# A hybrid decoder step on one core: the third k tile moves into the first array, and the squares of x are taken two chunks later

## The chip, the core and the metric

The kernel runs on one core of one Trainium2 chip. The metric is the device time of one execution in microseconds (us). Three executions of the kernel before took 1296.19, 1296.63 and 1296.79 us; the median is 1296.63 us.

## What is computed

One inference step of a one-layer decoder trunk for 264 tokens (256 of a prompt and 8 samples) with a model width of 2048. What matters here is the beginning:

```python
def rms_norm(x, g):
    xf = x.astype(jnp.float32)
    y = xf * lax.rsqrt(jnp.mean(xf * xf, axis=-1, keepdims=True) + EPS)
    return (y * g.astype(jnp.float32)).astype(x.dtype)

    xn = rms_norm(x, g_mix)
    z = xn @ w_in                     # 2048 x 3584, split among three mixers
    u_pool, u_lru, u_gel, c_a, c_b = z[..., :c0], z[..., c0:c1], ...
    # pooling mixer, RG-LRU mixer, conformer mixer: y_pool, y_lru, y_conf
    gates = jax.nn.sigmoid(xn @ w_gate + b_gate)
    x = x + (g_a * y_pool + g_b * y_lru + g_c * y_conf) @ w_out
    hid = jnp.square(jax.nn.relu(rms_norm(x, g_mlp) @ w_up))
    x = x + hid @ w_down              # then a last rms_norm
```

Everything is in float32. The outputs are the normalized tokens and the new states of the mixers.

## The kernel before, in words

**Three matmuls for one.** Every product is made from operands split in two: a weight block of 128 x 1024 is loaded into one of 6 buffers of `raw`, ScalarE (ACT) casts it to the rounded half `whi` (L176), and VectorE (DVE) subtracts that to get the rest `wlo` (L177). `whi` and `wlo` have 4 buffers each. TensorE (PE) then computes whi·x_hi, whi·x_lo and wlo·x_hi (L199 to L201). x has 16 k tiles of 128 features by 264 tokens; each is scaled by `g_mix` and split in two the same way into `A` (L298 on ACT, L299 on DVE).

**Chunks.** All weights form one list of chunks, and one Python loop runs over it: at chunk i, PE multiplies chunk i, while the splits of chunk i + 3 and of the x tiles that it needs are written out just ahead. Chunks 0 to 3 are the "wide" ones (one k tile by 1024 columns of `w_in`, 24 matmuls each, L981); from chunk 4 on a chunk is two k tiles by 512 columns, also 24 matmuls. Chunks 4 to 9 and 10 to 15 finish the same 1024 columns for the other 12 k tiles; when chunk 9 is done, four result banks are copied off by ACT (L400). The order on each engine is the order in which the loop writes the instructions out (a list of delayed functions, `later(n, fn)`, is emptied at the end of each chunk's turn); each engine runs its own list strictly in that order.

**Transfers.** All are issued by SyncE's queue (SP) in order. At first come four pieces of the array `head_dram`, which holds `g_mix` and, for k tiles 0 and 1, x and the weight row one behind the other (tile `first`, L160); then x tile 2 from `x_dram` (L157) and chunk 2 in two halves from `wall_dram` (L154), then x tiles and chunks in turn. From chunk 8 on, two chunks come in one transfer of 1 MB (L147; the pair of chunks 12 and 13 is one), which waits until DVE has read the buffers that it overwrites.

**The norm's factor.** Since the scale 1/rms belongs to a token, it is applied to results of `w_in`, not to x. For it, ACT squares x in four groups of four tiles (`x_squares`, L334; the first group in two instructions), DVE adds the groups (L338) and folds four tiles to one (L345, L346), `rms_parts` folds the 128 partitions in two halves with DVE and ACT in turn (L277, L278, L285, L281) into `parts`, and one matmul with a matrix of ones sums over the partitions (`sum_mm`, L273). That matmul is written into PE's list in the middle of chunk 13 (`if i == 13 and kt == 1: x_rms()`). Its result goes through Ln and Exp on ACT (L257) and four steps on DVE to `rstd`.

Of the kernel before, what the change touches and what calls it, by code (L numbers as in the profile page):

```python
# [16 lines left out]
P = 128  # L17
# [3 lines left out]
N = TP + TS  # L21
KD = D // P
# [24 lines left out]
CH = 1024  # L47
# [3 lines left out]
WARM = 7 * (512,)  # L51
AHEAD = 3
EARLY = 2
SINGLE = 1
WIDE = 4
TAIL = 6
# [4 lines left out]
ROW = N + CH  # L61
# [31 lines left out]
def hybrid_step(ctx: ExitStack, tc: tile.TileContext, head_in, x_in, par_in, st_in, row_in, wall, y_out, c_out, st_out):  # L93
    nc = tc.nc
# [8 lines left out]
    raw = cpool.tile([P, NRAW, CH], F32, name="raw")  # L103
    whi = cpool.tile([P, NHI, CH], F32R, name="whi")
    wlo = cpool.tile([P, NHI, CH], F32R, name="wlo")
    qtmp = cpool.tile([P, 16 * N], F32, name="qtmp", tag="Q")
    first = cpool.tile([P, KD + EARLY * ROW], F32, name="first")
    early = first[:, KD:].rearrange("p (k c) -> p k c", k=EARLY)
    X = cpool.tile([P, KD, N], F32, name="X")
# [4 lines left out]
    par = cpool.tile([P, NPAR], F32, name="par")  # L114
    st = cpool.tile([P, S_OUT], F32, name="st")
# [9 lines left out]
    def pv(name, i=None, n=1):  # L125
        a, b = PCOL[name]
        return par[:, a:b] if i is None else par[:, a + i:a + i + n]

    def acc():
        return psum.tile([P, 512], F32, name="acc", tag="acc")  # L130
# [11 lines left out]
    def dma_pair(p):  # L142
        s = (2 * p) % NRAW
        if p >= n_pairs:
            return
        if chunks[2 * p][3] == chunks[2 * p + 1][3] == CH and p < n_pairs - SINGLE:
            nc.sync.dma_start(raw[:, s:s + 2, :], wall[p].rearrange("p (a c) -> p a c", a=2))  # L147
        else:
            for h in range(2):
                if chunks[2 * p + h][3]:  # L150
                    dma_part(2 * p + h, 0, chunks[2 * p + h][3])

    def dma_part(c, a, b):
        nc.sync.dma_start(raw[:, c % NRAW, a:b], wall[c // 2, :, c % 2 * CH + a:c % 2 * CH + b])  # L154

    def dma_x(a, b):
        nc.sync.dma_start(X[:, a:b, :], x_in[:, a - EARLY:b - EARLY, :])  # L157

    def dma_first(a, b):
        nc.sync.dma_start(first[:, a:b], head_in[:, a:b])  # L160
# [1 line left out]
    def x_tiles(a, b):  # L162
        return early[:, a:b, :N] if b <= EARLY else X[:, a:b, :]

# [5 lines left out]
    def split(j, a=0, b=CH):  # L170
        if j >= len(chunks) or not chunks[j][3]:
            return
        h, lo = in_two(j)
        s = slice(a, min(b, chunks[j][3]))
        r = early[:, j, N + s.start:N + s.stop] if j < EARLY else raw[:, j % NRAW, s]
        nc.scalar.copy(h[:, s], r)  # L176
        nc.vector.tensor_tensor(lo[:, s], r, f(h[:, s]), op=ALU.subtract)  # L177
# [43 lines left out]
    def later(n, fn):  # L221
        delayed.append((now[0] + n, fn))
# [26 lines left out]
    def spend(**kw):  # L249
        for e, c in kw.items():  # L250
            credit[e] -= c
# [61 lines left out]
    warm, one = acc(), nc.const_aps.tensor(1.0, (P, P), BF16)  # L313
    for n in WARM:
        nc.tensor.matmul(warm[:, :n], one, nc.const_aps.tensor(1.0, (P, n), BF16), start=True, stop=True)
    for c, a, b in ((2, 2, 3), (3, 3, 4), (4, 4, 6), (5, 6, 8), (6, 8, 10), (7, 10, 12)):
        dma_x(a, b)
        for u, v in ((0, 512), (512, CH)) if c == 2 else ((0, CH),):
            dma_part(c, u, v)
    el = B[0].rearrange("p a n -> p (a n)")[:, :8 * (TP + 3)].rearrange("p (a n) -> p a n", a=8)  # L320
    nc.gpsimd.memset(el[:, :, 0:3], 0.0)
    nc.gpsimd.memset(vext[:, :, 0:30], 0.0)
# [4 lines left out]
    def x_tile(k):  # L327
        split_scaled(A[:, k, :], A[:, 16 + k, :], x_tiles(k, k + 1)[:, 0, :], first[:, k:k + 1], k < 2)

    def x_squares(j):  # L330

        t = sq4 if j == 0 else G[:, 4 * (j % 2):4 * (j % 2) + 4, :]
        for a, b in ((0, EARLY), (EARLY, 4)) if j == 0 else ((0, 4),):
            nc.scalar.activation(t[:, a:b, :], x_tiles(4 * j + a, 4 * j + b), AF.Square)  # L334
        spend(act=1.1)

        def add():
            nc.vector.tensor_tensor(sq4, sq4, t, op=ALU.add)  # L338
            spend(dve=1.25)

        if j:
            later(1, add)
# [11 lines left out]
    def softplus():  # L354
        sc = G[:, 8, :]
        t0, t1, t2, w, t4 = (sc[:, 8 * i:8 * i + 8] for i in range(5))
        lam = pv("lru_lambda")
        nc.scalar.activation(t0, lam, AF.Abs)
        nc.scalar.activation(w, t0, AF.Exp, scale=-1.0)
        nc.vector.tensor_scalar(t0, w, 2.0, None, op0=ALU.add)  # L360
        nc.vector.reciprocal(t1, t0)
        nc.vector.tensor_scalar(t4, lam, -1.0, 0.0, op0=ALU.mult, op1=ALU.max)
        eng = nc.gpsimd
        eng.tensor_tensor(t0, w, t1, op=ALU.mult)
        eng.tensor_tensor(t1, t0, t0, op=ALU.mult)
        terms = 10
        eng.memset(t2, 2.0 / (2 * terms + 1))
        for i in range(terms - 1, -1, -1):
            eng.tensor_tensor(t2, t2, t1, op=ALU.mult)
            eng.tensor_scalar(t2, t2, 1.0, 2.0 / (2 * i + 1), op0=ALU.mult, op1=ALU.add)  # L370
        eng.tensor_tensor(t2, t2, t0, op=ALU.mult)
        eng.tensor_tensor(t2, t2, t4, op=ALU.add)
        eng.tensor_scalar(sp[:, 0:8], t2, 4.0, 0.0, op0=ALU.mult, op1=ALU.add)
        eng.tensor_scalar(sp[:, 8:16], t2, -8.0, 0.0, op0=ALU.mult, op1=ALU.add)
# [600 lines left out]
    def wide_mm(k):  # L975

        hi, lo = whi[:, k % NHI, :], wlo[:, k % NHI, :]
        for ms in ((0, 1), (2, 3), (4, 5), (6, 7)) if k == 0 else (range(4), range(4, 8)):
            for w, x, start in ((hi, k, True), (hi, KD + k, False), (lo, k, False)):
                for m in ms:  # L980
                    nc.tensor.matmul(pair[m][:, :N], w[:, m * P:(m + 1) * P], sent(A[:, x, :]),  # L981
                                     start=start and k == 0, stop=False)

    def x_of(i):

        return [i] if i < WIDE else range(2 * i - WIDE, min(2 * i - WIDE + 2, KD))
# [17 lines left out]
    for i, ch in enumerate(chunks):  # L1004
        now[0] = i
        for k in x_of(i + AHEAD):
            x_tile(k)
        for a in (0, 512) if i < 3 else (0,):
            if i + AHEAD < len(chunks) - 1:
                split(i + AHEAD, a, a + (512 if i < 3 else CH))  # L1010
        if i == end - 2:
            split(len(chunks) - 1)
        if ch[0] == "wide":
            wide_mm(i)
        if i == 16:
            softplus()
            nc.gpsimd.tensor_scalar(gfin, pv("g_final"), -0.5, 0.0, op0=ALU.mult, op1=ALU.add)
        if i == 0:
            dma_x(12, 16)
        if i % 2 == 0:  # L1020
            dma_pair((i + 8) // 2)
        if i == 3:
            nc.sync.dma_start(par, par_in)
            nc.sync.dma_start(st[:, :S_IN], st_in)
        kind, gi, c, _ = ch
        if kind == "dense":
            rhs, fn = group(gi)
            n = groups[gi][2] // 2
            if i >= end:
                run_bg()  # L1030
                continue
            if c == 0:
                pss = [acc() for _ in range(4)] if gi > 2 else pair[4 * gi - 4:4 * gi]
                if groups[gi][:2] == ("w_down", 48) and groups[gi][3] == 3:
                    end_tiles()
            if i < end - 2:
                for kt in range(2):
                    if i == 13 and kt == 1:
                        x_rms()
                    for m in range(4):  # L1040
                        tile_mm(i, gi, c, kt, m, rhs, pss, c == n - 1 and kt == 1)
            elif i == end - 1:
                for m in range(4):
                    for b in range(4):
                        tile_mm(i - 1 + b // 2, gi, c - 1 + b // 2, b % 2, m, rhs, pss, b == 3)
            if c == n - 1:
                for m in range(4):
                    fn(m, pss[m])
                after(gi)
        elif kind == "lru":  # L1050
            for j in range(2):
                lru_gate_mm(2 * gi + j, i, j)
            if gi == 3:
                lru_tail()
        elif kind == "grp":
            grp_mm(i)
        if i == end - 2:
            nc.scalar.preload_act_table_set(ROOT)
        if i == 140:
            nc.sync.dma_start(st_out, st)  # L1060
        if end - 20 <= i < end - 4:
            for n in range(2):
                dma_turned(2 * (i - end + 20) + n)
        if end - 4 <= i < end:
            dma_rows(i - end + 4)
        if 5 <= i < 9:
            x_squares(i - 5)
        if i == 9:
            later(0, x_sum)
            later(1, lambda: rms_parts(sq4[:, 0, :]))  # L1070
        run_bg()
# [285 lines left out]
```

## Time and profile before

| what | us |
|---|---|
| median of three runs | 1296.63 |
| the profiled execution itself | 1296.88 |
| its span, first to last instruction | 1295.2 |
| PE busy | 1289.7 |
| DVE busy | 835.8 |
| ACT busy | 720.0 |

The profile is of one execution; its granted TensorE clock is 0.999. In the views, a row of the timeline gives the start, the duration, the engine, the line of the kernel and the tiles, and in brackets how long the engine had been idle and what released it. Instructions of one engine overlap by a little, so the distance from one start to the next is what an instruction costs its engine. The 1.7 us between the span and the time of the execution lie outside the instructions.

### The profile page before, as it was taken

To read this page: it belongs to the slowest core of one execution; us is meant where nothing else is said; L and a number is where in the kernel's file an instruction comes from. 1 tells how busy PE (TensorE), PEld (TensorE's weight loads), DVE (VectorE), ACT (ScalarE), POOL (GpSimd) and SP (SyncE) were. 2 spreads that over 40 slices of the span, in tenths; PEclk is the share of its full clock that TensorE was granted. 3 is DMA by queue.
4 is the path that set the end of the run, shared out by engine and by line. 5 is a ranking of instruction groups with operands and counts; after the bars stand their busy time and mean duration, and the time that the engine had idled before them with its cause. 6 is when DMAs were issued, how large, how long until landed. Compare 5 with 4: busy or idle time off the path is not lost.

```text
span 1295.2 us, 26872 instructions
## 1 busy us (share of the span) xinstructions
PE 1289.7 (100%) x11460; PEld 1286.1 (99%) x11460; DVE 835.8 (65%) x1064; ACT 720.0 (56%) x1034; POOL 122.1 (9%) x170
## 2 busy tenths in 40 slices
PE   9999999999999999999999999999999999999998
PEld 8999999999999999999999999999999999999998
DVE  6896898776776677666655455655455645465654
ACT  7767677667675655455544334543344533354455
POOL 0250010110102023131000000000000000001033
PEclk9999999999999999999999999999999999999999
DMA  9656566555565554655555555555555555555672
GB/s 342 219 184 203 186 212 201 196 196 195 197 228 195 192 197 162 229 195 195 197 195 196 196 196 195 196 196 196 195 196 195 196 195 196 195 196 196 207 221 93
DMA packets 44743, 257.91 MB, mean 199 GB/s; under 512 B 9824, under 2 KB 10848, under 8 KB 15312
## 3 DMA queue, kind: packets, MB, share of 16 engines
q1 hardware_dynamic: 44624, 256.21, 58.1%
q8 instruction: 89, 1.46, 0.4%
q14 instruction: 30, 0.25, 0.1%
HBM read 252.36 MB, written 3.22 MB: 197 GB/s over the span
## 4 chain that ended last, share of the span: by engine, by line
PE 99%; DMA 0%; DVE 0%; ACT 0%; issue 0%; DVEq 0%
PE acc L201 33%; PE acc L200 32%; PE acc L199 32%; PE acc L981 1%; PE acc L1103 1%; DMA first<-head_dram 0%; PE acc L1122 0%; DVE G L1200 0%; PE acc L1137 0%; DVE end L1190 0%; PE acc L273 0%; ACT whi L176 0%; PE acc L1118 0%; PE acc L1132 0%; DVE end L1173 0%
## 5 line engine op out<-in xcount | busy, mean ns | idle before, releaser
L177 DVE TENSOR_TENSOR wlo<-raw,whi 128x1024 fp32r<-128x1024 f32 (+2 forms) x479 | 585.3, 1224 | 439.4 <-ACT whi L176 433.6
L176 ACT CAST whi<-raw 128x1024 fp32r<-128x1024 f32 (+2 forms) x479 | 492.7, 1032 | 525.2 <-PE acc L200 479.2
L201 PE MATMUL acc<-A,wlo 128*128 128x264 f32 x1952 | 538.9, 276 | 0.0
L200 PE MATMUL acc<-A,whi 128*128 128x264 f32 x1952 | 538.8, 276 | 0.0
L199 PE MATMUL acc<-A,whi 128*128 128x264 f32 x1952 | 538.7, 276 | 0.0
L201 PEld LDWEIGHTS acc<-A,wlo 128*128 128x128 f32 x1952 | 368.9, 189 | 0.1
L199 PEld LDWEIGHTS acc<-A,whi 128*128 128x128 f32 x1952 | 368.9, 189 | 0.0
L200 PEld LDWEIGHTS acc<-A,whi 128*128 128x128 f32 x1952 | 368.9, 189 | 0.0
L199 PE MATMUL acc<-xn,whi 128*128 128x264 f32 x1024 | 282.6, 276 | 0.0
L200 PE MATMUL acc<-xn,whi 128*128 128x264 f32 x1024 | 282.6, 276 | 0.0
L201 PE MATMUL acc<-xn,wlo 128*128 128x264 f32 x1024 | 282.6, 276 | 0.0
L199 PEld LDWEIGHTS acc<-xn,whi 128*128 128x128 f32 x1024 | 193.5, 189 | 0.0
L201 PEld LDWEIGHTS acc<-xn,wlo 128*128 128x128 f32 x1024 | 193.5, 189 | 0.0
L200 PEld LDWEIGHTS acc<-xn,whi 128*128 128x128 f32 x1024 | 193.5, 189 | 0.0
L200 PE MATMUL acc<-Q,whi 128*128 128x264 f32 x620 | 171.1, 276 | 0.0
L199 PE MATMUL acc<-LH,whi 128*128 128x264 f32 x616 | 170.0, 276 | 0.0
L201 PE MATMUL acc<-LH,wlo 128*128 128x264 f32 x616 | 170.0, 276 | 0.0
L200 PEld LDWEIGHTS acc<-Q,whi 128*128 128x128 f32 x620 | 117.2, 189 | 0.0
L199 PEld LDWEIGHTS acc<-LH,whi 128*128 128x128 f32 x616 | 116.4, 189 | 0.0
L201 PEld LDWEIGHTS acc<-LH,wlo 128*128 128x128 f32 x616 | 116.4, 189 | 0.0
L832 POOL COPY G<-G 128x32 f32<-128x32 f32 x6 | 3.7, 641 | 590.5 <-ACT G L828 590.5
L591 ACT ACTIVATE G<-tmp,par 128x256 f32<-128x256 f32 x120 | 54.2, 498 | 2.8 <-DVE G L594 2.0
(235 smaller groups left out, 871.9 us busy)
## 6 DMA issues: line engine op xcount, KB each, us to landing
raw<-wall_dram SPq DMA_DIRECT2D x229, 1024.0 KB, 4.9
raw<-wall_dram SPq DMA_DIRECT2D x11, 512.0 KB, 4.2
raw<-wall_dram SPq DMA_DIRECT2D x7, 256.0 KB, 3.4
X<-x_dram SPq DMA_DIRECT2D x4, 264.0 KB, 8.2
so_dram<-st SPq DMA_DIRECT2D x1, 1018.0 KB, 9.4
st<-st_dram SPq DMA_DIRECT2D x1, 912.0 KB
y_dram<-G SPq DMA_DIRECT2D x3, 256.0 KB, 2.1
y_dram<-G SPq DMA_DIRECT2D x3, 208.0 KB, 2.4
```

Of the source, the lines that this page charges most:

```text
L176: nc.scalar.copy(h[:, s], r)
L177: nc.vector.tensor_tensor(lo[:, s], r, f(h[:, s]), op=ALU.subtract)
L199: nc.tensor.matmul(ps[:, :N], whi_t, xh, start=first, stop=False)
L200: nc.tensor.matmul(ps[:, :N], whi_t, xl, start=False, stop=False)
L201: nc.tensor.matmul(ps[:, :N], wlo_t, xh, start=False, stop=last)
L591: nc.scalar.activation(dst[:, ct, :TP], vext[:, ct, k:k + TP], AF.Copy, scale=par[:, w:w + 1])
L832: nc.gpsimd.tensor_copy(hid_last[:, m - KD + TAIL, :], t[:, N - TC:])
L981: nc.tensor.matmul(pair[m][:, :N], w[:, m * P:(m + 1) * P], sent(A[:, x, :]), start=start and k == 0, stop=False)
L1103: nc.tensor.matmul(ps[:size[g], :n], x, sent(w), start=s == 0 and not g * h, stop=s == 3 * TAIL - 1)
```

## The change

```diff
+HEAD = 3
     def dma_x(a, b):
-        nc.sync.dma_start(X[:, a:b, :], x_in[:, a - EARLY:b - EARLY, :])
+        nc.sync.dma_start(X[:, a:b, :], x_in[:, a - HEAD:b - HEAD, :])
...
-    for c, a, b in ((2, 2, 3), (3, 3, 4), (4, 4, 6), (5, 6, 8), (6, 8, 10), (7, 10, 12)):
+    for k in range(EARLY, HEAD):
+        row = head_in[:, KD + k * ROW:KD + (k + 1) * ROW]
+        nc.sync.dma_start(X[:, k, :], row[:, :N])
+        for a in (0, 512):
+            nc.sync.dma_start(raw[:, k, a:a + 512], row[:, N + a:N + a + 512])
+    for c, a, b in ((3, 3, 4), (4, 4, 6), (5, 6, 8), (6, 8, 10), (7, 10, 12)):
         dma_x(a, b)
-        for u, v in ((0, 512), (512, CH)) if c == 2 else ((0, CH),):
-            dma_part(c, u, v)
+        dma_part(c, 0, CH)
...
-        if 5 <= i < 9:
-            x_squares(i - 5)
-        if i == 9:
+        if 7 <= i < 11:
+            x_squares(i - 7)
+        if i == 11:
             later(0, x_sum)
             later(1, lambda: rms_parts(sq4[:, 0, :]))
...
-    head = np.concatenate([vec] + [... for k in range(EARLY)], 1)
+    head = np.concatenate([vec] + [... for k in range(HEAD)], 1)
```

The third x tile and the third weight row (chunk 2) are laid behind the first two in `head_dram` and are loaded from there, into the same buffers as before, by three transfers of the same sizes at the same places of SP's list. The four squares are written out at chunks 7 to 10 instead of 5 to 8, their sum at chunk 11 instead of 9, and `rms_parts` at chunk 12 instead of 10. The matmul over `parts` stays at chunk 13. No instruction is added or taken away; the new file has five more lines ahead of most code, so L176 becomes L177, L334 becomes L339 and so on.

ACT, from the cast of chunk 8 on (`whi<-raw` casts stand in the order of the chunks; the `128x528` and `128x1056` ones into `G` are the squares, `G<-acc` the four copies after chunk 9). Before:

```order
L176 CAST whi<-raw 128x1024
L334 ACTIVATE G<-first 128x528
L334 ACTIVATE G<-X 128x528
L298 ACTIVATE A<-X,first 128x264 x2
L176 CAST whi<-raw 128x1024
L334 ACTIVATE G<-X 128x1056
L176 CAST whi<-raw 128x1024
L334 ACTIVATE G<-X 128x1056
L176 CAST whi<-raw 128x1024
L334 ACTIVATE G<-X 128x1056
L176 CAST whi<-raw 128x1024
L400 COPY G<-acc 128x264 x4
```

The same place in the changed kernel, up to the last square:

```order
L177 CAST whi<-raw 128x1024
L299 ACTIVATE A<-X,first 128x264 x2
L177 CAST whi<-raw 128x1024 x2
L339 ACTIVATE G<-first 128x528
L339 ACTIVATE G<-X 128x528
L177 CAST whi<-raw 128x1024
L339 ACTIVATE G<-X 128x1056
L177 CAST whi<-raw 128x1024
L405 COPY G<-acc 128x264 x4
L339 ACTIVATE G<-X 128x1056
L177 CAST whi<-raw 128x1024
L339 ACTIVATE G<-X 128x1056
```

The squares stand behind the casts of chunks 10, 11, 12 and 13 instead of 8, 9, 10 and 11; the four copies now come ahead of the last two squares.

DVE, from the difference of chunks 9 and 10 on to the last step of `rms_parts`. Before:

```order
L177 TENSOR_TENSOR wlo<-raw,whi 128x1024 x2
L338 TENSOR_TENSOR G<-G 128x1056
L177 TENSOR_TENSOR wlo<-raw,whi 128x1024
L338 TENSOR_TENSOR G<-G 128x1056
L177 TENSOR_TENSOR wlo<-raw,whi 128x1024
L338 TENSOR_TENSOR G<-G 128x1056
L345 TENSOR_TENSOR G<-G 128x528
L346 TENSOR_TENSOR G<-G 128x264
L177 TENSOR_TENSOR wlo<-raw,whi 128x1024
L278 TENSOR_TENSOR fold<-G,fold 64x264
L281 TENSOR_TENSOR parts<-fold,parts 64x264
L177 TENSOR_TENSOR wlo<-raw,whi 128x1024 x3
```

Now:

```order
L178 TENSOR_TENSOR wlo<-raw,whi 128x1024 x4
L343 TENSOR_TENSOR G<-G 128x1056
L178 TENSOR_TENSOR wlo<-raw,whi 128x1024
L343 TENSOR_TENSOR G<-G 128x1056
L178 TENSOR_TENSOR wlo<-raw,whi 128x1024
L343 TENSOR_TENSOR G<-G 128x1056
L350 TENSOR_TENSOR G<-G 128x528
L351 TENSOR_TENSOR G<-G 128x264
L178 TENSOR_TENSOR wlo<-raw,whi 128x1024
L279 TENSOR_TENSOR fold<-G,fold 64x264
L282 TENSOR_TENSOR parts<-fold,parts 64x264
L178 TENSOR_TENSOR wlo<-raw,whi 128x1024
```

The whole group of adds and folds stands two differences later: the first add behind chunk 12's difference instead of chunk 10's, the last step into `parts` behind chunk 15's instead of chunk 13's.

PE, in the middle of chunk 13, before:

```order
L199 MATMUL acc<-A,whi 128x264
L200 MATMUL acc<-A,whi 128x264
L201 MATMUL acc<-A,wlo 128x264
L273 MATMUL acc<-parts,ones_r 128x264
L199 MATMUL acc<-A,whi 128x264
```

and now:

```order
L200 MATMUL acc<-A,whi 128x264
L201 MATMUL acc<-A,whi 128x264
L202 MATMUL acc<-A,wlo 128x264
L274 MATMUL acc<-parts,ones_r 128x264
L200 MATMUL acc<-A,whi 128x264
```

Nothing moved on PE: the matmul that reads `parts` stands between the same two matmuls of chunk 13.

More of the change, by code (lines that the diff above doesn't have):

```diff
@@ L1319 @@
                     dynamic_dma_scratch_size=1024)
-    head = np.concatenate([vec] + [t for k in range(EARLY) for t in (x[:, k], a["w_in"][0][k * P:(k + 1) * P, 512:512 + CH])], 1)
-    arrays = {"head_dram": np.ascontiguousarray(head), "x_dram": np.ascontiguousarray(x[:, EARLY:]), "par_dram": par, "st_dram": st,
+    head = np.concatenate([vec] + [t for k in range(HEAD) for t in (x[:, k], a["w_in"][0][k * P:(k + 1) * P, 512:512 + CH])], 1)
+    arrays = {"head_dram": np.ascontiguousarray(head), "x_dram": np.ascontiguousarray(x[:, HEAD:]), "par_dram": par, "st_dram": st,
               "row_dram": np.ascontiguousarray(np.concatenate(
```

## The prediction

> **What bounds the kernel now.** I read the busy times and the chain of waits first, then PE's counts over long stretches, then the timelines of PE, ACT and DVE around chunks 8 to 13.
>
> ```profile
> PE 1289.7 (100%) x11460; PEld 1286.1 (99%) x11460; DVE 835.8 (65%) x1064; ACT 720.0 (56%) x1034; POOL 122.1 (9%) x170
> PE 99%; DMA 0%; DVE 0%; ACT 0%; issue 0%; DVEq 0%
> 45.00:245.00 200.00, 200.00 (x1780) 200.00 (x1780) 164.99 (x242) 143.62 (x229) 33.29 (x44) 1.00 0.60 200
> 1045.00:1245.00 200.00, 200.00 (x1781) 200.00 (x1780) 111.11 (x133) 93.12 (x116) 13.56 (x24) 1.00 0.59 198
> ```
>
> The chain that ends last is PE alone. From 45 us on every 200 us hold 1780 matmuls (the first and the last of six such stretches are shown), 0.112 us apart: PE waits for nothing there. So time can be won only where PE waits in the first 45 us, and a new wait there is paid in full, since no later idle time of PE could take it back. The waits of the opening:
>
> ```profile
> 29.60 0.28 PE L200 MATMUL acc<-A,whi 128*128 128x264 f32 x1
> 29.73 0.38 PE L201 MATMUL acc<-A,wlo 128*128 128x264 f32 x1
> 29.95 0.28 PE L199 MATMUL acc<-A,whi 128*128 128x264 f32 x1
> ...
> 41.65 0.28 PE L201 MATMUL acc<-A,wlo 128*128 128x264 f32 x1
> 41.76 0.29 PE L273 MATMUL acc<-parts,ones_r 128*128 128x264 f32 x1
> ```
>
> At 29.60 the second, at 29.73 the third matmul of chunk 9 stands, the first that reads its `wlo`. From 29.60 to 29.95 are 0.35 us where two steps of 0.112 are due: 0.12 us lost. From 29.95 to 41.65 are 104 steps of 0.1125, none lost, and at 41.76 the matmul over `parts` follows its neighbour without a gap.
>
> Who was late, and how much room `parts` had, stands on ACT and DVE:
>
> ```profile
> 24.55 1.05 ACT L176 CAST whi<-raw 128x1024 fp32r<-128x1024 f32 x1 [1.64 <-DMA raw<-wall_dram]
> 25.50 0.64 ACT L334 ACTIVATE G<-first 128x528 f32<-128x528 f32 x1
> ...
> 26.58 0.91 ACT L298 ACTIVATE A<-X,first 128x264 fp32r<-128x264 f32 x2
> 27.39 1.03 ACT L176 CAST whi<-raw 128x1024 fp32r<-128x1024 f32 x1
> 28.32 1.08 ACT L334 ACTIVATE G<-X 128x1056 f32<-128x1056 f32 x1
> 29.31 1.03 ACT L176 CAST whi<-raw 128x1024 fp32r<-128x1024 f32 x1
> ...
> 33.85 1.03 ACT L176 CAST whi<-raw 128x1024 fp32r<-128x1024 f32 x1
> 34.78 1.21 ACT L400 COPY G<-acc 128x264 f32<-128x264 f32 x4
> 35.86 1.08 ACT L176 CAST whi<-raw 128x1024 fp32r<-128x1024 f32 x1
> ```
>
> ```profile
> 25.63 1.22 DVE L177 TENSOR_TENSOR wlo<-raw,whi 128x1024 fp32r<-128x1024 f32 x1 [1.73 <-ACT whi L176]
> ...
> 28.45 1.23 DVE L177 TENSOR_TENSOR wlo<-raw,whi 128x1024 fp32r<-128x1024 f32 x1 [0.44 <-ACT whi L176]
> ...
> 32.68 1.22 DVE L177 TENSOR_TENSOR wlo<-raw,whi 128x1024 fp32r<-128x1024 f32 x1
> 33.82 1.25 DVE L338 TENSOR_TENSOR G<-G 128x1056 f32<-128x1056 f32 x1
> 34.99 1.22 DVE L177 TENSOR_TENSOR wlo<-raw,whi 128x1024 fp32r<-128x1024 f32 x1
> 36.12 1.25 DVE L338 TENSOR_TENSOR G<-G 128x1056 f32<-128x1056 f32 x1
> ...
> 38.50 1.22 DVE L177 TENSOR_TENSOR wlo<-raw,whi 128x1024 fp32r<-128x1024 f32 x1
> ...
> 40.53 0.43 DVE L281 TENSOR_TENSOR parts<-fold,parts 64x264 fp32r<-64x264 f32 x1 [0.48 <-ACT parts L285]
> ```
>
> Chunk 9's difference runs from 28.45 to 29.68; the matmul that it releases takes effect at 29.84 (29.95 less one step), 0.16 later. That is PE's price for being released by DVE. `parts` is done at 40.96 (40.53 + 0.43); with 0.16 the sum could start at 41.12 and starts at 41.76, so there is **0.64 us of room**. The change takes two chunks, 5.4 us of PE's time, from this chain and leaves its reader where it was.
>
> **The change, part by part.**
>
> *The third k tile in the first array.* Three transfers keep size and place; only their source differs. What hides it:
>
> ```profile
> 8.79 1.27 ACT L176 CAST whi<-raw 128x256 fp32r<-128x256 f32 x3
> 10.51 1.06 PE L981 MATMUL acc<-A,whi 128*128 128x264 f32 x8
> 12.01 1.14 ACT L176 CAST whi<-raw 128x512 fp32r<-128x512 f32 x2 [1.53 <-DMA raw<-wall_dram]
> 13.21 0.50 PE L981 MATMUL acc<-A,whi 128*128 128x264 f32 x3
> ```
>
> Chunk 2's cast starts back to back with ACT's work before it at 8.79, and PE reads it from 10.51. Chunk 3's, the next in the queue, waits for its transfer until 12.01; its first half is cast by 12.6 (12.01 + 1.14/2) and read at 13.21, 0.6 us later. A faster source gains nothing, since PE does not wait there; a slower one costs nothing until the three transfers lose 0.6 us. I take 0; bounds 0 and +0.9 us (their 644 KB take 1.5 us at the 435 GB/s of a window quoted below; if they took twice that, 1.5 more, less the room of 0.6).
>
> *The squares out of the way of chunk 9.* Behind chunk 8's cast (its next at 25.50, 0.95 later) the two squares take 1.08 (25.50 to 26.58), then the x tiles 0.81. Without the squares chunk 9 is cast at 26.31 instead of 27.39 and its difference comes at 27.58, behind chunk 8's (26.77) and two x tiles (taken at ACT's 0.81): done at 28.8, 0.9 earlier. PE's 0.12 us goes. It would be the whole gain.
>
> *The chain to `parts`, two chunks later.* I follow ACT by the distances of the rows: a cast 0.93 (27.39 to 28.32), a square 0.99 (28.32 to 29.31), the first square 1.08, four copies 1.08. Chunk 9's cast 26.31, chunk 10's 27.24, first square 28.17, chunk 11's cast 29.25, second square 30.18, chunk 12's cast from 31.17 as far as ACT goes. But chunk 12 must have landed:
>
> ```profile
> 24.00:26.00 2.00, 2.00 (x20) 2.00 (x19) 0.37 (x1) 1.45 (x2) 0.00 (x0) 1.00 1.07 435
> ...
> 23.11 0.33 SPq L147 DMA_DIRECT2D raw<-wall_dram  x1
> ...
> raw<-wall_dram SPq DMA_DIRECT2D x1, 1024.0 KB, 8.9
> ```
>
> Its transfer is issued at 23.11 (the wait ahead of it is for chunk 7, which nothing here moves) and takes 8.9 us, behind the queue: 32.0. (Chunks 10 and 11 are one transfer behind the pair whose landing released ACT at 24.55; 1 MB at the 435 GB/s of that window is 2.4 us, so 27.0, in time for 27.24.) So chunk 12's cast starts at 32.05 and ends at 33.08; then the copies from 32.98, third square 34.06, chunk 13's cast 35.05 to 36.08, fourth square 35.98, chunk 14's cast 36.97 to 38.00.
>
> DVE, a difference 1.14 (32.68 to 33.82), an add 1.17 (33.82 to 34.99), 0.03 behind a cast that it waits for: chunk 12's difference 33.11, first add 34.25, chunk 13's difference waits for its cast until 36.11, second add 37.25, chunk 14's difference 38.42, third add **39.55**. From the third add to the end of `parts` are the same steps as before, with one difference among them (38.50): 36.12 to 40.96, 4.84 us. So `parts` is done at 44.39 and the sum starts at **44.55, 2.79 us after the 41.76 of now**. PE has reached it by 41.64 and stands for 2.9 us.
>
> Behind the waiting matmul stand the other half of chunk 13 and all of PE's list; ACT and DVE have chunks 14 and 15 split by then. What needs the sum's result moves less than PE does:
>
> ```profile
> 43.25 0.47 ACT L257 ACTIVATE rstd<-acc,eps 128x264 f32<-128x264 f32 x1
> ```
>
> Ln starts at 43.25 now; then at 44.84 at the earliest (44.55 + 0.29), 1.6 later, while PE's need of free banks moves by 2.8. Nothing further is late.
>
> **The sum**: against the profiled execution 1296.88 + 2.79 = 1299.7 us; against the median, 0.25 lower, **1299.4 us** (the 0.12 won at chunk 9 is inside, since the sum's start hangs on `parts` alone). That is +0.22%. A measurement here can tell about 0.2%, 2.6 us, from no change; the forecast stands just beyond it, at 1299.2.
>
> Bounds: the unsure term is when the pair of chunks 12 and 13 lands. If earlier, ACT's own 31.17 would hold, and then the copies, which need chunk 9 done on PE (29.95 + 21 steps = 32.3 for its last start now, 0.12 earlier then, some 0.3 for its end): from 32.5 instead of 32.98, so at most 0.5 less, +2.3. Later by as much: +3.3. I keep 32.0, the only landing on record. Nothing in the rows lets the chain come back to its present time.
>
> **The rivals.**
>
> *A: the same wait, but under 2.6 us.* The pair lands by 31.8 or earlier; +2.3 to +2.55, 1298.9 us. For it: the pair ahead of it was the only thing that ACT waited for at 24.55, and a queue that drains a little sooner is enough. Against it: one landing, at 32.0.
>
> *B: PE comes back at half clock.* The rows of PE's first matmuls:
>
> ```profile
> 0.84 3.14 PE L315 MATMUL acc<-const-bfloat16-1.0 128*128 128x512 bf16 x7 [0.84 <-PEq L1318]
> 4.10 1.24 PE L981 MATMUL acc<-A,whi 128*128 128x264 f32 x4
> 6.46 0.61 PE L981 MATMUL acc<-A,whi 128*128 128x264 f32 x4
> ```
>
> Four matmuls at 6.46 take 0.61 us together, the same four at 4.10 took 1.24, and PE had been at work since 0.84. If a gap of 2.9 us put PE back to twice the step and that held as long as at first (0.84 to 6.46, 5.6 us), half of that is lost: +2.8 on top, 1302.2 us. Against it: the present trace has no gap to learn from after 6.24.
> [...]
>
> *C, the other side: not slower.* ACT, free of squares at chunk 8, runs far enough ahead for `parts` to be ready when PE comes at 41.64; PE keeps the 0.12 won, 1296.5 us. It decides at `parts` done by 41.48, 2.9 us earlier than I have it. Against it: DVE's own work from chunk 12's difference to `parts` is 1.14 + 1.17 + 1.14 + 1.17 + 1.14 + 4.84 = 10.6 us without any wait, so that difference would have to start by 30.9, behind a cast that starts by 29.8, over 2 us ahead of its transfer's landing.
>
> *D: the third tile lands late* and PE waits at chunk 3: up to +0.9 on top, 1300.3 us. Against it: the transfers are as large as before and stand at the same places.
>
> **How the numbers follow.** The forecast 0.58, A 0.24, B 0.11, C 0.04, D 0.03. Of the forecast's share 0.50 lies beyond 2.6 us and 0.08 within; with B and D slower has 0.64. A, that 0.08 and C's 0.12 us gain are no change to a measurement: together 0.36, less 0.02 that I give to a gain over 0.2%, which no row supports: same 0.34, faster 0.02. The range goes from 1298.5 (the lower bound +2.3, less 0.4 for distances taken from one execution) to 1301.2 (+3.3, D's 0.9 and 0.4 for the distances); it leaves out C, most of B and little of A, about 0.16.
>
> **What would show it.** The changed profile should have PE idle, or one stretched step, for about 2.9 us ahead of the sum over `parts` near 41.7, and the end of `parts` near 44.4, with chunk 12's cast released by its transfer near 32.0. Chunk 9's difference should end near 28.8 and the 0.12 us loss at its third matmul should be gone. Chunk 2's and chunk 3's first matmuls should stand at 10.5 and 13.2. I am wrong if the sum starts within a microsecond of 41.8, if PE's steps behind it are 0.2 us apart (B), if chunk 12's cast starts back to back near 31.2 (A), or if PE's count in later stretches falls under 1780 in 200 us.

## The result, and the profile after

The changed kernel takes 1299.69 us (median of ten executions, 1299.09 to 1301.92) against 1296.70 us before (ten, 1296.18 to 1297.12): 1.0028 times as long, 95% interval 1.0020 to 1.0037, or 3.0 us more. The ten times lie in two groups: six from 1299.09 to 1299.80 (median 1299.37) and four from 1301.13 to 1301.92, with nothing between; the kernel before has one group. Two executions of the kernels below (3373 and 1489 us) and two of the kernel before beside them (1329 and 3871 us) took far longer than the rest and are in no range, group or ratio here.

The profiled execution took 1299.09 us, 2.21 us more than the profiled one before (1296.88), so it belongs to the first group. From its page, the busy times and the engines of the chain that ended last; behind them the first 200 us after the opening (columns: stretch, its length, busy time and count of PE, of its weight loads, of DVE, ACT and POOL, clock, share of the DMA engines, GB/s):

```profile
PE 1289.5 (99%) x11460; PEld 1285.8 (99%) x11460; DVE 835.8 (64%) x1064; ACT 720.2 (56%) x1034; POOL 122.3 (9%) x170
PE 96%; DMA 2%; DVE 1%; ACT 0%; SPq 0%; issue 0%; DVEq 0%; ACTq 0%
...
45.00:245.00 200.00, 200.00 (x1780) 200.00 (x1779) 163.37 (x239) 143.94 (x229) 33.11 (x43) 1.00 0.57 195
```

PE's work is the same, and its count per 200 us too. What is new is that the chain leaves PE: 2% of the span are transfers and 1% DVE. The place where it comes back to PE, in PE's timeline of the changed kernel:

```profile
41.26 0.28 PE L202 MATMUL acc<-A,wlo 128*128 128x264 f32 x1
43.88 0.36 PE L274 MATMUL acc<-parts,ones_r 128*128 128x264 f32 x1 [2.34 <-DVE parts L282]
44.08 0.28 PE L200 MATMUL acc<-A,whi 128*128 128x264 f32 x1
```

The matmul over `parts` was due at 41.37 (41.26 and one step of 0.112) and takes effect at 43.97 (44.08 less one step): **2.60 us of PE lost**, released by the last step of `parts` on DVE. Before, it took effect at 41.76, and 43.97 - 41.76 is 2.21 us, all of the difference between the two profiled executions (PE reached the sum 0.39 us earlier this time, at 41.37 instead of 41.76, so 2.60 us of wait cost it 2.21). What made `parts` late, on ACT and then on DVE in the same profile:

```profile
23.76 1.04 ACT L177 CAST whi<-raw 128x1024 fp32r<-128x1024 f32 x1 [1.64 <-DMA raw<-wall_dram]
...
25.53 1.98 ACT L177 CAST whi<-raw 128x1024 fp32r<-128x1024 f32 x2
...
31.33 1.04 ACT L177 CAST whi<-raw 128x1024 fp32r<-128x1024 f32 x1 [0.82 <-DMA raw<-wall_dram]
32.28 1.21 ACT L405 COPY G<-acc 128x264 f32<-128x264 f32 x4
33.37 1.11 ACT L339 ACTIVATE G<-X 128x1056 f32<-128x1056 f32 x1
34.35 1.07 ACT L177 CAST whi<-raw 128x1024 fp32r<-128x1024 f32 x1
...
44.28 0.48 ACT L258 ACTIVATE rstd<-acc,eps 128x264 f32<-128x264 f32 x1
```

```profile
26.79 2.35 DVE L178 TENSOR_TENSOR wlo<-raw,whi 128x1024 fp32r<-128x1024 f32 x2
...
32.41 1.23 DVE L178 TENSOR_TENSOR wlo<-raw,whi 128x1024 fp32r<-128x1024 f32 x1 [1.63 <-ACT whi L177]
...
38.90 1.25 DVE L343 TENSOR_TENSOR G<-G 128x1056 f32<-128x1056 f32 x1
...
43.31 0.43 DVE L282 TENSOR_TENSOR parts<-fold,parts 64x264 fp32r<-64x264 f32 x1 [0.48 <-ACT parts L286]
```

Chunk 12's cast waits for its transfer until 31.33; from there the chain runs to the third add at 38.90 and the end of `parts` at 43.74. Chunk 9's difference is the first of the two from 26.79 on, 1.7 us earlier than before (28.45); 0.8 of that is this execution's transfers (chunk 8's cast at 23.76 instead of 24.55), 0.9 the squares that no longer stand ahead.

### The profile page after: what moved, and what is told of

It reads as the page before. It is cut to its first block, busy times and chain, and to the rows that moved or that the text cites. A ratio compares the mean times of both kernels' runs of the same rounds, so it can differ in the third digit from the quotient of the medians.

```text
span 1297.4 us, 26871 instructions
## 1 busy us (share of the span) xinstructions
PE 1289.5 (99%) x11460; PEld 1285.8 (99%) x11460; DVE 835.8 (64%) x1064; ACT 720.2 (56%) x1034; POOL 122.3 (9%) x170
## 4 chain that ended last, share of the span: by engine, by line
PE 96%; DMA 2%; DVE 1%; ACT 0%; SPq 0%; issue 0%; DVEq 0%; ACTq 0%
PE acc L200 32%; PE acc L201 32%; PE acc L202 32%; DMA raw<-wall_dram 2%; PE acc L1108 1%; DVE wlo L178 0%; DVE G L343 0%; ACT whi L177 0%; SPq L161 0%; PE acc L1127 0%; ACT G L405 0%; DVE G L1205 0%; ACT G L339 0%; DVE A L300 0%; SPq L321 0%
## 5 line engine op out<-in xcount | busy, mean ns | idle before, releaser
L177 ACT CAST whi<-raw 128x1024 fp32r<-128x1024 f32 (+2 forms) x479 | 492.7, 1031 | 528.2 <-PE acc L201 475.4
```

## The experiments

Two things are to be explained: the wait, and the second group of times, about 2 us above the first. My theory for the first is the prediction's: a chain two chunks later before a reader that stays. The rivals are a share of the moved third tile, and a cost per chunk of delay without any room. For the second group there are two candidates: PE coming back at half clock from its idle time (the prediction's rival B), or a wait that is simply longer in some executions, say by late transfers. Sums below count from 1296.6 to 1296.7 us, the median of the kernel before beside each run.

**One part alone.** The squares two chunks later, with the third tile where it was (only these lines of the diff):

```diff
-        if 5 <= i < 9:
-            x_squares(i - 5)
-        if i == 9:
+        if 7 <= i < 11:
+            x_squares(i - 7)
+        if i == 11:
```

> The changed kernel with the third k tile put back where it was before: only the squares come two chunks later. Theory (the sum over the partitions waits for its operand and nothing else changes): as the changed kernel, +2.2 to +3.1 us in a run without further loss, matmul over parts about 2.6 us behind its due time. Rival (the new place of the third tile costs a part of it): under +1.5 us.

Measured: 1299.38 us, ratio 1.0026 (1.0015 to 1.0038); four of seven times from 1299.12 to 1299.38, three from 1300.87 to 1301.18. In its PE timeline:

```profile
44.07 0.36 PE L273 MATMUL acc<-parts,ones_r 128*128 128x264 f32 x1 [2.65 <-DVE parts L281]
```

The same wait, and the same two groups. The third tile alone, with the squares in their old place (the rest of the diff):

> Only the third k tile in the first array; the squares stand where they were. Theory: no change, within 0.5 us of the kernel before; the matmul over parts at about 41.8 us or earlier by what the opening varies, 0.1 us still lost at chunk 9. Rival (third tile late): +0.3 to +0.9 us, a late first matmul of chunk 2 or 3.

Measured: 1296.68 us, ratio 1.0001 (0.9992 to 1.0009); ten of eleven times from 1296.15 to 1297.03, and one of 1298.23, which was not profiled.

```profile
41.22 0.28 PE L202 MATMUL acc<-A,wlo 128*128 128x264 f32 x1
41.33 0.28 PE L274 MATMUL acc<-parts,ones_r 128*128 128x264 f32 x1
```

and on DVE, the last step into `parts`:

```profile
39.92 0.43 DVE L282 TENSOR_TENSOR parts<-fold,parts 64x264 fp32r<-64x264 f32 x1 [0.48 <-ACT parts L286]
```

No wait, no cost and no gain from the new array. The whole change in time belongs to the squares. One detail went against the expectation: in this profile chunk 9's third matmul is not late, although the squares stand in its way as before. Here that difference starts at 27.84 on DVE instead of 28.45, 0.61 us earlier, while PE is only 0.43 earlier (41.33 against 41.76 at the sum): the loss of 0.12 us in the profile before belongs to how that execution's opening ran.

**The size of the delay.** The changed kernel with one chunk of delay instead of two:

```diff
-        if 7 <= i < 11:
-            x_squares(i - 7)
-        if i == 11:
+        if 6 <= i < 10:
+            x_squares(i - 6)
+        if i == 10:
```

> The changed kernel with the squares one chunk later than before instead of two. Theory: by the same distances parts are done near 42.2 us, the sum waits about 0.8 us and the time is +0.6 us (0 to +1.1 with the landing of chunks 12 and 13); no run with a further loss of 2 us. Rival (each chunk of delay costs the same, half of the change): +1.3 to +1.5 us.

Measured: 1297.14 us, +0.5 us (eleven times from 1296.71 to 1297.89, one group); ratio 1.0004 (0.9995 to 1.0013).

```profile
41.28 0.28 PE L202 MATMUL acc<-A,wlo 128*128 128x264 f32 x1
42.09 0.36 PE L274 MATMUL acc<-parts,ones_r 128*128 128x264 f32 x1 [0.53 <-DVE parts L282]
42.28 0.27 PE L200 MATMUL acc<-A,whi 128*128 128x264 f32 x1
```

Due at 41.39, in effect at 42.17: 0.78 us lost. One chunk costs about a fifth of what two cost (0.5 against 2.7 us, the lower group of the changed kernel), since the first of them uses up the room. The rival's half of the change (+1.3 to +1.5) is out.

**The reader moved too.** The changed kernel with the matmul over `parts` at the head of chunk 15:

```diff
-                    if i == 13 and kt == 1:
+                    if i == 15 and kt == 0:
                         x_rms()
```

In this kernel the LRU's first convolution comes behind the second and behind what reads it, so a part of the values differs; its time is read for the wait alone.

> The changed kernel with the matmul over parts moved too, to the head of chunk 15 (due near 45.7 us). Theory: no wait ahead of it, since parts are done by 44.4, and PE keeps the 0.1 us of chunk 9: -0.1 us, within 0.3 us of the kernel before, no run with a further loss. Rival (the factor comes too late for what follows): a new wait of PE at chunk 16, for the bank that the sum has used, or later, and +0.5 us or more.

Measured: 1296.78 us, +0.1 us, all eleven times from 1296.48 to 1297.04.

```profile
45.35 0.28 PE L202 MATMUL acc<-A,wlo 128*128 128x264 f32 x1
45.46 0.29 PE L274 MATMUL acc<-parts,ones_r 128*128 128x264 f32 x1
```

The squares stand two chunks later as in the changed kernel, yet wait and second group are both gone. The later squares cost nothing of themselves; the reader that stayed does.

**The landing of chunk 12.** The changed kernel with the transfer of the states behind the pair of chunks 12 and 13:

```diff
         if i == 3:
             nc.sync.dma_start(par, par_in)
+        if i == 5:
             nc.sync.dma_start(st[:, :S_IN], st_in)
```

> The changed kernel with the 912 KB transfer of the states issued two chunks later, behind the pair of chunks 12 and 13 instead of ahead of it. Theory (chunk 12's landing is a term of the wait): the pair lands some 2 us earlier, chunk 12's cast starts back to back, the copies behind it wait for PE's chunk 9 until about 32.5 us; the wait is some 0.3 us shorter than in the changed kernel, +1.9 to +2.5 us, and runs with a further loss are rarer. Rival (the landing does not matter): as the changed kernel, +2.2 to +3.1 us with 4 of 10 runs at +4.6 us.

Measured: 1298.63 us, +2.0 us, ratio 1.0019 (1.0010 to 1.0028); eight times from 1298.22 to 1299.01, and 1300.22 and 1301.23.

```profile
30.48 1.03 ACT L177 CAST whi<-raw 128x1024 fp32r<-128x1024 f32 x1
31.42 1.20 ACT L405 COPY G<-acc 128x264 f32<-128x264 f32 x4
...
43.00 0.36 PE L274 MATMUL acc<-parts,ones_r 128*128 128x264 f32 x1 [1.79 <-DVE parts L282]
```

Chunk 12's cast now follows the square ahead of it without a wait, at 30.48 instead of 31.33, and the sum follows at 43.00 instead of 43.88: the landing is a term, 0.85 us at chunk 12's cast for 0.88 us at the sum; the eight lower times have their median at 1298.5, 0.8 below the six of the changed kernel. The copies did not wait for PE at 32.5 as I had bounded it; they start at 31.42, so that bound was too high. The second group is still there; two of ten against four of ten is too small a difference to call it rarer.

**The second group: doses of idle time.** Here the kernel before is used, with unused adds of DVE ahead of the folds, so that only the length of PE's wait changes. The three kernels have 2, 4 and 7 of them:

```diff
-    def rms_parts(total):
+    def rms_parts(total, more=0):
+        for _ in range(more):
+            nc.vector.tensor_tensor(G[:, 0:4, :], G[:, 20:24, :], G[:, 20:24, :], op=ALU.add)
         rms_fold(total)
```

> The kernel before with two more adds of 128x1056 on DVE (their result is not used) ahead of the last folds into parts, 1.17 us each. Theory: the sum waits 2 x 1.17 - 0.64 = 1.7 us, PE's clock is not touched: +1.7 us in all runs, spread as small as that of the kernel before (under 1 us). If gaps of any length bring back the half clock in some runs: some runs at +3.4 us or more.

> The same with four more adds: the sum waits 4 x 1.17 - 0.64 = 4.0 us. Theory (a gap long enough puts PE back to half clock): +4.0 us and 1.7 to 2.8 us more in nearly all runs, +5.7 to +6.8 us, matmuls 0.225 us apart for 3.4 us or more behind the gap. Rival (the runs at +4.6 us of the changed kernel have another cause, such as late transfers): +4.0 us, matmuls 0.11 us apart from the first.

> The kernel before with seven unused adds ahead of the last folds into parts (1.28 us each, as four of them measured): the sum waits about 7 x 1.28 - 1.0 = 8 us. Theory (an idle PE goes back to half clock): every run loses 1.7 to 2.8 us on top, +9.7 to +10.8 us, and the profile shows the matmuls behind the gap 0.225 us apart for some microseconds. Rival (the loss on top comes from something else): +8 us and matmuls 0.11 us apart from the first.

The 1.7 and 2.8 us of these expectations agree with times on record by then: 1.7 is the distance between the medians of the two groups of the squares-only kernel (1299.25 and 1300.92), 2.8 the whole spread of the changed one (1299.09 to 1301.92). 3.4 us at twice the step lose 1.7.

Two adds: 1298.05 us, +1.4 us, all eleven times from 1297.76 to 1299.03, none near +3.4 (the spread is 1.3 us, where I expected under 1). Four adds: 1302.05 us, +5.4 us, a little under the +5.7 that I expected at least; one time of 1300.12 (+3.5), four from 1301.92 to 1303.39. Seven adds: 1306.90 us, +10.3 us, all four from 1306.68 to 1307.14. The profile of the four-add kernel is of its one low time:

```profile
44.91 0.36 PE L273 MATMUL acc<-parts,ones_r 128*128 128x264 f32 x1 [3.17 <-DVE parts L281]
45.10 0.28 PE L199 MATMUL acc<-A,whi 128*128 128x264 f32 x1
```

and that of the seven-add kernel:

```profile
49.67 0.56 PE L273 MATMUL acc<-parts,ones_r 128*128 128x264 f32 x1 [8.11 <-DVE parts L281]
50.02 0.42 PE L199 MATMUL acc<-A,whi 128*128 128x264 f32 x1
50.24 0.43 PE L200 MATMUL acc<-A,whi 128*128 128x264 f32 x1
...
53.10 0.43 PE L201 MATMUL acc<-A,wlo 128*128 128x264 f32 x1
53.32 0.32 PE L199 MATMUL acc<-A,whi 128*128 128x264 f32 x1
53.48 0.28 PE L200 MATMUL acc<-A,whi 128*128 128x264 f32 x1
53.59 0.28 PE L201 MATMUL acc<-A,wlo 128*128 128x264 f32 x1
```

After an idle time of 3.2 us this execution went on at full step (0.11 us). After 8.1 us the matmuls come 0.22 us apart from 50.02 to 53.32 (15 steps in 3.30 us, where 1.69 were due) and then 0.11 again: 1.6 us lost behind the gap, and about 0.1 more on the sum itself. By these doses no execution of eleven falls behind with two adds, four of five do with four (the low time is the fifth), and four of four with seven.

**Filling the wait.** The changed kernel, with eleven unused matmuls ahead of the one over `parts` (`fill` is 11 for this sum and 0 for the others):

```diff
         ps = acc()
+        for _ in range(fill):
+            nc.tensor.matmul(ps, nc.const_aps.tensor(1.0, (P, P), BF16), nc.const_aps.tensor(1.0, (P, 512), BF16),
+                             start=True, stop=True)
```

> The changed kernel with eleven unused matmuls of 512 bf16 columns (0.216 us each, 2.4 us) ahead of the matmul over parts, so that PE works through most of its wait. Theory (an idle PE is what brings the half clock): the wait itself stays, +2.2 to +3.1 us, and no run has a loss on top; the spread falls from 2.8 us to under 1.2 us. Rival (the loss on top does not come from the idle PE): 4 of 10 runs still near +4.6 us.

Measured: 1299.72 us, +3.1 us, ten times from 1299.11 to 1300.74, spread without a gap.

```profile
41.44 0.28 PE L202 MATMUL acc<-A,wlo 128*128 128x264 f32 x1
41.56 2.58 PE L275 MATMUL acc<-const-bfloat16-1.0 128*128 128x512 bf16 x11
43.90 0.36 PE L277 MATMUL acc<-parts,ones_r 128*128 128x264 f32 x1
44.10 0.27 PE L200 MATMUL acc<-A,whi 128*128 128x264 f32 x1
```

The sum is as late as in the changed kernel (43.90 against 43.88), so the wait is paid. The eleven matmuls themselves last from 41.56 to 43.90, 0.213 us each, and the sum follows without idle time: they take up the whole wait and would hold PE that long even with `parts` ready. But none of ten times reaches 1301, and none has a mean granted clock under 0.999, where the four of the second group had 0.998. In all, none of ten has the loss, against nine of nineteen executions with the same wait unfilled (four of ten, three of seven, and both of the next two). The spread is 1.6 us, wider than the 1.2 I expected; the times of 1300.1 to 1300.7 were not profiled, and why they are higher than the rest stays open.

**Two more profiles of the changed kernel**, unchanged:

> The changed kernel once more, for a second profile of it. Theory (two parts: the wait, and in some runs the half clock behind it): the wait ahead of the sum over parts 2.3 to 3.3 us, by where the pair of chunks 12 and 13 lands; if its time is near 1301 us, some 15 matmuls behind the gap 0.22 us apart, if near 1299.4, all 0.11 us apart. Rival: a time near 1301 with 0.11 us steps behind the gap.

> The same, for a third profile of the changed kernel: again the steps behind the gap tell the two kinds of time apart.

They took 1303.95 and 1301.24 us, beside 1296.87 for the kernel before. The first:

```profile
42.63 0.28 PE L202 MATMUL acc<-A,wlo 128*128 128x264 f32 x1
45.77 0.56 PE L274 MATMUL acc<-parts,ones_r 128*128 128x264 f32 x1 [2.86 <-DVE parts L282]
46.12 0.42 PE L200 MATMUL acc<-A,whi 128*128 128x264 f32 x1
...
51.84 0.30 PE L202 MATMUL acc<-A,wlo 128*128 128x264 f32 x1
51.97 0.28 PE L200 MATMUL acc<-A,whi 128*128 128x264 f32 x1
```

and the second:

```profile
41.85 0.28 PE L202 MATMUL acc<-A,wlo 128*128 128x264 f32 x1
44.39 0.56 PE L274 MATMUL acc<-parts,ones_r 128*128 128x264 f32 x1 [2.26 <-DVE parts L282]
44.74 0.42 PE L200 MATMUL acc<-A,whi 128*128 128x264 f32 x1
...
47.60 0.37 PE L201 MATMUL acc<-A,whi 128*128 128x264 f32 x1
47.81 0.28 PE L202 MATMUL acc<-A,wlo 128*128 128x264 f32 x1
```

This is the half clock of rival B in the changed kernel itself: steps of 0.22 us instead of 0.11, and a mean granted clock of 0.997 and 0.998 against 0.999 in the first profile of this kernel. In the second, 14 steps take 3.07 us (44.74 to 47.81) where 1.58 were due, 1.5 us lost; the sum takes effect at 44.52 (44.74 less a slow step of 0.22), 2.76 us after the 41.76 of the profile before; together 4.3 of its 4.4 us. In the first, 27 steps take 5.85 us (46.12 to 51.97) where 3.04 were due, 2.8 us lost; PE also reached the sum a microsecond later (due at 42.75 against 41.76), so that it took effect at 45.90, 4.1 us later than before; 6.9 of its 7.1 us.

Why one execution falls back and another does not is not shown. The length of the idle time alone does not tell them apart: 2.86 and 2.26 us (these two profiles) and 8.11 us (seven adds) were followed by steps of 0.22 us, but 2.34 us (the first profile of the changed kernel), 2.65 us (squares only) and 3.17 us (four adds) by steps of 0.11. Nor is it shown why the slow steps go on for 5.85 us in the first of these two profiles and for 3.07 us in the second.

**A version with room.** One chunk of delay for the squares, and one for the reader; the LRU's first convolution is put into its queue at once, so that it keeps its place:

```diff
-        if 7 <= i < 11:
-            x_squares(i - 7)
-        if i == 11:
+        if 6 <= i < 10:
+            x_squares(i - 6)
+        if i == 10:
...
-                    if i == 13 and kt == 1:
+                    if i == 14 and kt == 1:
                         x_rms()
...
-        later(1, lambda: lru_conv(range(4)))
+        lru_conv(range(4))
```

> The changed kernel with the squares one chunk later than before and the matmul over parts one chunk later too (middle of chunk 14, due near 44.1 us; the first convolution of the LRU is put into its queue at once, so that it stands ahead of the second as before). Theory: parts are done near 42 us, nothing waits, PE keeps what it lost at chunk 9: 0 to -0.3 us against the kernel before, no run with a loss on top. Rival (what follows the factor has no room for 2.7 us): PE waits at chunk 16 or later, +0.5 us or more.

Measured: 1296.83 us, ratio 1.0001 (0.9992 to 1.0010).

```profile
44.37 0.28 PE L202 MATMUL acc<-A,wlo 128*128 128x264 f32 x1
44.48 0.29 PE L274 MATMUL acc<-parts,ones_r 128*128 128x264 f32 x1
...
41.83 0.43 DVE L282 TENSOR_TENSOR parts<-fold,parts 64x264 fp32r<-64x264 f32 x1 [0.48 <-ACT parts L286]
```

`parts` is done at 42.26, 2.2 us before its reader, and nothing waits. The few tenths that I expected as a gain do not show in the times: this version equals the kernel before, it does not beat it.

## Why the prediction was right, and where it was not

**The third tile at nothing: right.** Alone it measured 1296.68 us, and in the profile after the first matmuls of chunks 2 and 3 stand at 10.32 and 13.02, where I had 10.5 and 13.2.

**The room of 0.64 us: right in kind, one execution's size.** With the third tile alone, `parts` would have let the sum start at 40.51 (its last DVE step ended at 40.35, and 0.16 for the release) where it was due at 41.33: 0.82 us. The 0.16 was a little small for this matmul: in the profile after, it takes effect 0.23 us behind the end of `parts` (43.74 to 43.97), which leaves 0.75. The two-add kernel lost 1.4 us instead of the 1.7 that 0.64 gave.

**The 0.12 us at chunk 9: a loss of that one execution.** With the squares back in its way, the loss was absent in another profile. I called it the whole possible gain; it is less than that, and the version with room shows no gain at all.

**The chain to `parts`, two chunks later: right, step by step, but for its start.** I had chunk 12's cast start at 32.05 and the third add at 39.55, 7.50 us later; the profile has 31.33 and 38.90, 7.57 later. From there to the end of `parts` it has the 4.84 us that I took over (38.90 to 43.74). The mis-sized term is the landing of the pair of chunks 12 and 13: 32.0 by the one on record, 31.3 in the profile after. The 8.9 us from issue to landing were right, and are the same there; it is the issue that came at 22.33 instead of 23.11, right behind chunk 7's difference on DVE (which ended at 22.31 instead of 23.08). Nothing in the change moves that step, as I said; this execution's opening ran 0.8 us earlier, and with the states moved the issue stands at 22.41. Chunk 8's cast, which waits for its own transfer, starts anywhere from 23.76 to 25.66 in the profiles before and after, the one with the states moved and the two extra ones. So the profiled execution lost 2.21 us against the one before where I had 2.79. Other executions landed nearer to mine: the second extra profile has its sum 2.76 us later, and the six lower times have their median 2.7 us above the kernel before. The bound that I put on an earlier landing (copies held by PE's chunk 9 until 32.5) was wrong: with the states moved the copies started at 31.42.

**Nothing further is late: right.** Ln moved from 43.25 to 44.28, by 1.0 us, less than PE's 2.2, and the counts per 200 us are as before.

**Rival B, the half clock: its chance failed.** I gave it 0.11 and 2.8 us. It came in four of the ten timed executions and in both of the extra profiles, at 1.8 to 2.6 us by the distance of the two groups, and at 1.5 and 2.8 us behind the gap in the extra profiles. It adds to the wait rather than replacing it, and since it comes in under half of the timed ones, the median stayed in the first group, at the upper end of it. Had one more of the ten had it, the median would have stood near 1300.4, with two more near 1301.1. So the forecast of 1299.4 us holds for the executions at full step; that the median of 1299.69 lies near it too is luck, with the loss in four of ten. The 0.11 was my estimate: that a gap of 2.9 us is unlikely to do harm was not shown by any row of the profile before. For a gap of 2.3 to 2.9 us a chance of about one half fits (nine of nineteen executions).

**How long a gap does no harm.** The forecast gave harm at 2.9 us of idle PE a chance of 0.11. The profiles differ: idle times of 2.26 and 2.86 us brought PE back at half step, and 2.34, 2.65 and 3.17 us did not. So no length of a harmless gap between 2.3 and 3.2 us can be read from these runs; one and the same kernel falls into two groups (1299.09 to 1299.80 and 1301.13 to 1301.92 us).

**Rivals A, C, D.** A (the wait under 2.6 us) is what the profiled execution shows, but not the median. C is out, since `parts` came 2.6 us late for PE, and D, since the third tile alone cost nothing.

## What to carry to other kernels

When a chain of small steps on two engines is moved later, look for the instruction on the bounding engine that reads its end, and move it by as much: the room in front of it is part of the schedule (here under a microsecond, with 5.4 us moved). Where PE waits nowhere else, as here (1780 matmuls per 200 us in both kernels), such a wait is paid in full (2.21 us later at the sum, 2.21 us more in the profiled execution) and is found by following the other engines' queues, transfers included, from one row to the next. Take the issue of a transfer, and with it its landing, as a range and not as a number (the issue stood at 22.33, 22.41 and 23.11 in three profiles here), and price an idle PE with what its clock may do afterwards (1.5 and 2.8 us more in the two extra profiles).

## What the runs showed of the hardware

The half clock behind a gap was not expected to matter at this length. By PE's idle time in the profiles: no second group at 0.5 and 0.8 us (0 of 22 timed executions), two of ten at 1.8, four of ten and three of seven at 2.3 to 2.7, four of five at 3.2, four of four at 8.1 us. These are idle times of one profile each, so the steps are approximate. At 2.3 to 3.2 us the length alone did not decide: steps of 0.22 us followed 2.26 and 2.86 us, steps of 0.11 followed 2.34, 2.65 and 3.17. In the slow steps a matmul of 264 columns takes 0.22 us instead of 0.1125. They went on for 3.07 and 5.85 us in the two extra profiles and for 3.30 us in the seven-add one. With eleven unused matmuls in the gap none of ten executions had the loss (all under 1301 us, with a mean granted clock of 0.999 or 1.0).

The 1 MB transfer of chunks 12 and 13 took 8.9 us from issue to landing in the profile before (issued at 23.11) and in the one after (at 22.33).
